# A new table of 61 queue-order pairs in place of 39, in a two-layer hybrid encoder on one core

## The chip, the core and the metric

The kernel runs on one core of a Trainium2 chip. The core has five instruction streams that run side by side and meet only at semaphores: TensorE (PE, with its weight loads shown apart as PEld), VectorE (DVE), ScalarE (ACT), GpSimd (POOL) and SyncE (SP), which here issues nearly all DMAs. Each stream works strictly in the order in which it was written: an instruction that waits holds up everything behind it on its own engine. The metric is the time of one execution on the device in microseconds; less is better. The time of a kernel is the median of several executions.

## The reference

The program is the trunk of an encoder: 512 tokens (a grid of 8 rows by 64 columns) and 16 meta tokens, width 1024, two layers, float32. Cut to what matters:

```python
def hybrid_layer(x, ...):                       # x: 528 x 1024
    h = rms_norm(x, norm_g)
    qa, ka, va, za, qb, kb, vb, zb, ga, gb = split_cols(h @ w_in)      # 1024 x 5376
    qa = rope(rms_norm(qa)); ka = rope(rms_norm(ka))                   # 8 query heads, 2 key heads
    oa = gqa_attention(qa, ka, va) * silu(za)                          # over all 528 keys
    ob = neighbourhood_attention(qb, kb, vb, rpb) * silu(zb)           # 8 heads, 8 x 16 window + meta keys
    mixed = sigmoid(ga) * (oa @ w_o_attn) + sigmoid(gb) * (ob @ w_o_na)
    return x + mixed @ w_out

def reference(x, meta_tokens, ...):
    h = concat([meta_tokens, x])
    for i in range(2):
        h = hybrid_layer(h, ...)
    return rms_norm(h, final_norm_g)[16:]
```

## The kernel before

**Products.** Features lie on the partitions, tokens on the free axis. Every dense product is made of three matmuls per tile: a weight tile is split into a rounded high part `whi` (a cast on ACT, L291) and the rest `wlo` (a subtraction on POOL, L292), the activations into `hh` and `hl`, and PE adds `whi*hh + whi*hl + wlo*hh` in one PSUM bank (L376 to L378). A chunk of 128 output features takes 24 such matmuls per span of tokens: 256 and 272 columns in layer 0 (tiles named like `pp0_11_256`: layer, chunk, first token), 512 in layer 1. Two banks `pp` take turns. Weight halves of 256 KB come by DMA through five buffers `raw`.

**The two attentions** run in the gaps between these chunks. After each span of a product a counter ticks, and steps that are due at that tick are written into the program. The global attention works in units of one head and 256 queries: scores `S` (L607, L608) in one PSUM tile of two banks, their scaled copy with its maximum on DVE (L889, output `P`), exponentials on ACT (L893), a transposition on DVE and by a DMA to DRAM (`turn`) and back, a split into `pth` (ACT) and `ptl` (DVE, L245), and sums `av` on PE (L957) that close with the meta keys `ga` (ACT L948, POOL L950). The windowed attention works by head: a bias tile of 480 KB is loaded (L1026), scores `Sb` go into the same PSUM tile `S`, DVE adds the bias and takes the extreme (L1042, statistic `stb`), ACT exponentiates (L1044), PE transposes (`ta`, `tb`, `tc`, `tm`, and `vtb`, `vtc` for the values) into two PSUM banks tagged `tp`, ACT and DVE split the results (`tah`/`tal`, `tbh`/`tbl`, `mm`, `na`, `VB`), and PE sums `avb` (L1104, eleven matmuls). `ob` and `oa` are the gated results (L825, L829), `mg` the merge gates, `y` the products with the output projections, `za` and `zb` the SiLU gates, `KA` the stacked keys of the global attention, `KB` and `QB` keys and queries of the windowed one.

**What sets the order.** The kernel is written against a planner: instructions are recorded in program order with their dependences, and the planner lays each engine's queue out by priority and by the times that it expects of each instruction; it adds all semaphores. The order on the chip is fixed then. Three things steer it: a few blocks of high priority, `issue_after` (what the block records comes behind a given instruction on its engine), and the table `BEHIND` with `queue_order` (called at the end, L1320 and on). For each engine, `BEHIND` holds pairs `(a, n, b, m)`: the n-th instruction of that engine (counted from 0 in program order) that writes tile `a` is queued behind the m-th one that writes tile `b`. The pair adds no semaphore; it only binds the order of the queue:

```python
kind = mybir.DependencyInfo(mybir.DependencyClass.NoSync, mybir.DependencyReason.DATA)
for engine, pairs in BEHIND.items():
    for a, n, b, m in pairs:
        tc.add_manual_dep(traced[engine, a, n], traced[engine, b, m].name, kind, reason="queue order")
```

Names of tiles carry their place: `avb0_3` is the sum of layer 0, windowed head 3; `S1_3_0_1` the scores of layer 1, head 3, unit 0, second half of its queries. The profile leaves these numbers out (it prints `avb`, `S`), so an instruction is found there by its place among those of its name.

Of the kernel before, what the change touches and what calls it, by code (L numbers as in the profile page):

```python
# [66 lines left out]
    "Activation": (  # L67
# [3 lines left out]
    ),  # L71
    "DVE": (
# [4 lines left out]
    ),  # L77
# [5 lines left out]
    ),  # L83
    "Pool": (
        ("wl6KB", 1, "gb0", 0), ("wlo0_17_1", 0, "zb0_1", 0), ("wlo1_38_1", 0, "zb1_3", 0),
    ),
    "SP": (
        ("turn1_2_1", 0, "QB1_2a", 0),
    ),
}  # L90

# [1276 lines left out]
```

## Time and profile before

| | us |
|---|---|
| median of 3 runs | 826.21 |
| lowest, highest | 824.33, 827.37 |
| the profiled execution | 826.77 |
| its span, first to last instruction | 824.7 |
| mean clock granted to PE, share of full speed | 0.999 |
| PE / PEld busy in the span | 812.2 / 756.4 |
| DVE / ACT / POOL busy in the span | 511.2 / 474.1 / 419.3 |

The profile shows one execution. A row of the timeline reads: start in us from the span's start, length in us, engine, line of the kernel, operation, output tile <- input tiles, shapes, count, and in brackets the idle time of the engine just before the row and what ended it. Rows of neighbouring instructions of one kind are merged (x3). In the view of waits a row reads: who waited <- for whom, us in total, number of waits, the longest. Matmuls are pipelined, so their lengths overlap; from the start of one to the start of the next is what a matmul takes of PE.

### The profile page before, as it was taken

To read this page: it belongs to the slowest core of one execution; us is meant where nothing else is said; L and a number is where in the kernel's file an instruction comes from. 1 tells how busy PE (TensorE), PEld (TensorE's weight loads), DVE (VectorE), ACT (ScalarE), POOL (GpSimd) and SP (SyncE) were. 2 spreads that over 40 slices of the span, in tenths; PEclk is the share of its full clock that TensorE was granted. 3 is DMA by queue.
4 is the path that set the end of the run, shared out by engine and by line. 5 is a ranking of instruction groups with operands and counts; after the bars stand their busy time and mean duration, and the time that the engine had idled before them with its cause. 6 is when DMAs were issued, how large, how long until landed. Compare 5 with 4: busy or idle time off the path is not lost.

```text
span 824.7 us, 16080 instructions
## 1 busy us (share of the span) xinstructions
PE 812.2 (98%) x5662; PEld 756.4 (92%) x5662; DVE 511.2 (62%) x1152; ACT 474.1 (57%) x1137; POOL 419.3 (51%) x362
## 2 busy tenths in 40 slices
PE   9999999999999999999999999999998999999997
PEld 9999999999999999999988989998987788888886
DVE  7566777796885662455547657676766755343733
ACT  8745677577865664433445557666757756534422
POOL 1654454454553544655754644554635456555841
PEclk9999999999999999999999999999999999999999
DMA  8347474567655563435555575666776455653502
GB/s 296 105 133 214 144 210 138 166 211 196 177 160 175 163 209 116 145 101 171 150 121 138 142 226 157 195 175 173 186 231 156 150 184 155 188 194 100 190 2 103
DMA packets 113249, 134.99 MB, mean 164 GB/s; under 512 B 31889, under 2 KB 66193, under 8 KB 113169
## 3 DMA queue, kind: packets, MB, share of 16 engines
q1 hardware_dynamic: 112448, 132.90, 54.8%
q8 instruction: 45, 0.74, 0.4%
q10 hardware_dynamic: 720, 1.06, 0.3%
q14 instruction: 36, 0.29, 0.1%
HBM read 98.50 MB, written 21.84 MB: 146 GB/s over the span
## 4 chain that ended last, share of the span: by engine, by line
PE 85%; DVE 5%; DMA 3%; ACT 3%; issue 2%; SPq 1%; POOL 0%; POOLq 0%; DVEq 0%; ACTq 0%
PE pp L378 18%; PE pp L376 18%; PE pp L377 18%; PE y L377 4%; PE y L378 4%; PE y L376 3%; PE av L957 3%; PE avb L1104 2%; PE S L607 2%; PE S L608 2%; DMA bias<-in_bias_dram 2%; PE pf L1287 2%; PE pf L1286 2%; PE pf L1288 2%; PE pp L496 2%
## 5 line engine op out<-in xcount | busy, mean ns | idle before, releaser
L292 POOL TENSOR_TENSOR wlo<-raw,whi 128x512 fp32r<-128x512 f32 x210 | 286.6, 1373 | 287.4 <-ACT whi L291 233.2
L376 PE MATMUL pp<-hh,whi 128*128 128x256 f32 (+2 forms) x1040 | 325.2, 313 | 0.0
L378 PE MATMUL pp<-hh,wlo 128*128 128x256 f32 (+2 forms) x1040 | 324.2, 312 | 0.0
L377 PE MATMUL pp<-hl,whi 128*128 128x256 f32 (+2 forms) x1040 | 323.3, 311 | 0.0
L378 PEld LDWEIGHTS pp<-hh,wlo 128*128 128x128 f32 x1040 | 195.8, 188 | 10.3
L377 PEld LDWEIGHTS pp<-hl,whi 128*128 128x128 f32 x1040 | 195.7, 188 | 9.3
L376 PEld LDWEIGHTS pp<-hh,whi 128*128 128x128 f32 x1040 | 195.9, 188 | 8.6
L291 ACT CAST whi<-raw 128x512 fp32r<-128x512 f32 x210 | 128.7, 619 | 110.4 <-PE pp L377 43.1
L950 POOL TENSOR_TENSOR ga<-pm,ga 32x128 fp32r<-32x128 f32 x64 | 39.5, 618 | 70.7 <-ACT ga L948 46.3
L919 DVE STREAM_TRANSPOSE P<-P 128x512 f32<-128x512 f32 x64 | 46.4, 725 | 29.7 <-ACT P L893 29.3
L1183 DVE TENSOR_TENSOR mg<-pp,rbc 128x256 f32<-128x256 f32 (+2 forms) x48 | 24.7, 515 | 47.8 <-PE pp L378 47.2
L889 DVE CUSTOM_DVE_ANT_0 P<-S,r 128x528 f32<-128x528 f32 x64 | 44.8, 701 | 15.2 <-PE S L608 14.7
L245 DVE TENSOR_TENSOR ptl<-P,pth 128x512 fp32r<-128x512 f32 x64 | 50.3, 800 | 4.4 <-ACT pth L244 4.2
L893 ACT ACTIVATE P<-P,st 128x528 f32<-128x528 f32 x64 | 47.2, 737 | 1.7
L1044 ACT ACTIVATE bias<-bias,stb 128x208 f32<-128x208 f32 (+1 forms) x64 | 31.0, 485 | 22.6 <-DVE stb L1042 22.5
L1184 ACT ACTIVATE mg<-mg 128x256 f32<-128x256 f32 (+2 forms) x48 | 23.6, 492 | 28.8 <-DVE mg L1183 28.5
L244 ACT CAST pth<-P 128x512 fp32r<-128x512 f32 x64 | 39.2, 613 | 0.5 <-DMA P<-turn 0.4
L377 PE MATMUL pp<-mx,whi 128*128 128x272 f32 (+1 forms) x128 | 36.4, 285 | 0.0
L376 PE MATMUL pp<-mx,whi 128*128 128x272 f32 (+1 forms) x128 | 36.4, 284 | 0.0
L378 PE MATMUL pp<-mx,wlo 128*128 128x272 f32 (+1 forms) x128 | 36.4, 284 | 0.0
L892 ACT ACTIVATE st<-st 128x1 f32<-128x1 f32 x64 | 12.9, 202 | 39.1 <-DVE st L889 38.6
L957 PE MATMUL av<-pth,VA 128*128 128x256 f32 x128 | 34.1, 288 | 0.0
(534 smaller groups left out, 1724.8 us busy)
## 6 DMA issues: line engine op xcount, KB each, us to landing
raw<-in_w_dram SPq DMA_DIRECT2D x210, 256.0 KB
turn<-P SPq DMA_DIRECT2D x32, 528.0 KB
P<-turn SPq DMA_DIRECT2D x128, 128.0 KB
bias<-in_bias_dram SPq DMA_DIRECT2D x16, 480.0 KB
KB<-KB SPq DMA_DIRECT2D x24, 272.0 KB
rawl<-in_w_dram SPq DMA_DIRECT2D x16, 256.0 KB
x<-in_xT_dram SPq DMA_DIRECT2D x8, 264.0 KB
xr<-in_xT_dram SPq DMA_DIRECT2D x8, 264.0 KB
```

Of the source, the lines that this page charges most:

```text
L244: split_at["hi"] = nc.scalar.copy(hi, src)
L245: split_at["any"] = nc.vector.tensor_sub(lo, src, hi.bitcast(F32))
L291: cast = nc.scalar.copy(hi, raw)
L292: sub = nc.gpsimd.tensor_sub(lo, raw, hi.bitcast(F32))
L376: nc.tensor.matmul(ps, wh, rh[:, a:b], start=i == 0, stop=False)
L377: nc.tensor.matmul(ps, wh, rl[:, a:b], start=False, stop=False)
L378: nc.tensor.matmul(ps, wl, rh[:, a:b], start=False, stop=i == n - 1)
L889: newest["max"] = nc.vector.tensor_tensor_reduce(p[:n], joined(S)[:n], scale[:n].to_broadcast([n, NTOK]), 1.0, -3e38, ALU.mult, ALU.max, s ...
L893: nc.scalar.activation(p[:n], p[:n], AF.Exp, bias=st[:n, 1:2], scale=1.0, accum_out=st[:n, 2:3] if total is None else total)
L919: nc.vector.transpose(c["both"][:n, a:b], c["both"][:n, a:b])
L950: nc.gpsimd.tensor_sub(tm[64 + 32 * t:96 + 32 * t, n * t:n * (t + 1)], m, tm[:32, :n].bitcast(F32))
L957: nc.tensor.matmul(c["av"], rows2(c["t"][i][0]), c["t"][i][1], start=i == 0, stop=i == 8)
```

## The change

The table `BEHIND` is replaced by one of 61 pairs, made over three cases of durations of the instructions. All 39 pairs of the old table stand in the new one; 22 are new (8 on PE, 7 on DVE, 5 on POOL, 1 on ACT, 1 on SP). Nothing else is changed: the same instructions, tiles and DMAs. The new pairs are:

```diff
     "Activation": (
+        ("st0_2_1_1", 0, "whi0_13_1", 0),
     "DVE": (
+        ("KA1l1", 0, "P1_0_0", 0), ("VB20_0", 1, "qr0_1", 1), ("mg1_34_5", 0, "ptl1_5_1_0", 0),
+        ("ob0_2", 4, "mm0", 12), ("ptl0_1_0_0", 0, "kb0_2", 0), ("q0_3", 2, "ob0_3", 3),
+        ("za1_3", 0, "ptl1_3_1_0", 0),
     "PE": (
+        ("S1_3_0_1", 0, "avb1_3", 4), ("S1_3_0_1", 0, "avb1_3", 5), ("av1_2_1", 1, "pp1_17_256", 9),
+        ("avb0_3", 6, "pp0_8_0", 3), ("avb0_3", 9, "S0_2_1_1", 1), ("sm0_7", 0, "pp0_35_256", 0),
+        ("tc0_0", 0, "pp0_19_0", 15), ("vtc0_0", 0, "pp0_11_256", 19),
     "Pool": (
+        ("KB1_20", 0, "za1_0", 0), ("ga0", 7, "wlo0_20_1", 0), ("ga0", 51, "wlo1_36_1", 0),
+        ("ga0", 52, "wlo1_36_1", 0), ("wlo0_21_0", 0, "ga0", 10),
     "SP": (
+        ("Q20_1", 2, "KB0_11", 0),
```

More of the change, by code (lines that the diff above doesn't have):

```diff
@@ L69 @@
         ("mg0_26_0", 0, "pth0_6_1_0", 0), ("mg1_26_2", 0, "ga0", 64), ("na0", 6, "pth0_1_1_2", 0),
[1 row of a table removed]
[2 rows of a table added]
     ),
     "DVE": (
[4 rows of a table removed]
[5 rows of a table added]
     ),
     "PE": (
[4 rows of a table removed]
[7 rows of a table added]
     ),
     "Pool": (
-        ("wl6KB", 1, "gb0", 0), ("wlo0_17_1", 0, "zb0_1", 0), ("wlo1_38_1", 0, "zb1_3", 0),
+        ("KB1_20", 0, "za1_0", 0), ("ga0", 7, "wlo0_20_1", 0), ("ga0", 51, "wlo1_36_1", 0), ("ga0", 52, "wlo1_36_1", 0),
+        ("wl6KB", 1, "gb0", 0), ("wlo0_17_1", 0, "zb0_1", 0), ("wlo0_21_0", 0, "ga0", 10), ("wlo1_38_1", 0, "zb1_3", 0),
     ),
     "SP": (
-        ("turn1_2_1", 0, "QB1_2a", 0),
+        ("Q20_1", 2, "KB0_11", 0), ("turn1_2_1", 0, "QB1_2a", 0),
     ),
```

23 rows, old and new, of the table BEHIND are left out of this document.

## The prediction, made before the change was run

> **What bounds the kernel now.** I read the page of the profile first, then the view of who waited for whom, limited to TensorE (PE), then the timeline around each place that the new table touches.
>
> ```profile
> span 824.7 us, 16080 instructions
> PE 812.2 (98%) x5662; PEld 756.4 (92%) x5662; DVE 511.2 (62%) x1152; ACT 474.1 (57%) x1137; POOL 419.3 (51%) x362
> ```
>
> PE is busy for 812.2 of 824.7 us and no other engine passes 62%. An order of instructions can't make a matmul shorter, so all that it can win lies in the 12.5 us in which PE stands still. The waits view (line, what it waited for, us in total, times, longest) splits them:
>
> ```profile
> PE S L607 <- DVE stb L1042: 2.7, 2, 2.1
> PE warm L188 <- DVE one L194: 1.1, 1, 1.1
> PE y L377 <- DVE ob L245: 0.7, 1, 0.7
> PE y L377 <- DVE oa_3b L245: 0.4, 1, 0.4
> PE avb L1104 <- DVE na L850: 0.4, 2, 0.3
> PE tm L180 <- DVE tal L245: 0.4, 1, 0.4
> PE vtc L791 <- DVE tal L245: 0.3, 1, 0.3
> PE avb L1104 <- ACT tbh L244: 0.3, 1, 0.3
> PE S L607 <- DVE st L889: 0.2, 1, 0.2
> ```
>
> That is 6.5 us, 1.1 of them before the first matmul; the other 6.0 are the tail behind the last matmul and what rounding leaves, and no pair touches the tail. So 5.4 us, in 10 waits, are within reach. Each costs a little more than its idle time: the profile draws a matmul of 256 columns 0.28 long while the next one starts 0.12 later (rows below: 573.70 to 573.81), so a wait of w delays PE by w + 0.16. Ten waits make 5.4 + 1.6 = 7.0 us, and one that shows only at the weight load (first place below) adds 0.3: **7.3 us, 0.9%, is all that any order could take away here.**
>
> **The change part by part.** No instruction is added or removed. All 39 old pairs stay and 22 come in: 8 on PE, 7 on DVE, 5 on POOL, 1 on ACT, 1 on the DMA queue of SP. I followed each new pair (a behind b) to its two instructions: in every one a now stands ahead of b, by 1 to 16 instructions. So each asks for a local move. Five of them meet a wait.
>
> First place: the transposes vtc of head 0 (vtc0_0) go 8 matmuls back, behind pp0_11_256 number 19. They wait for a PSUM bank that DVE's tal frees.
>
> ```profile
> 92.43 0.28 PE L377 MATMUL pp<-hl,whi 128*128 128x272 f32 x1
> 92.78 0.27 PEld L791 LDWEIGHTS vtc<-ident,vb 128*80 128x80 f32 x3 [0.29 <-PE pp L378]
> 92.81 0.50 PE L791 MATMUL vtc<-ident,vb 128*80 128x128 f32 x3
> ```
>
> Start to start is 0.38 where 0.12 is the pace: 0.26 is lost. Eight matmuls are 8 x 0.12 = 1.0 us of ready work, so the wait goes: **-0.26**. Queued behind vtc0_0 are the transposes tb and tc; what they make, with VB, is read by avb, which the chain of work has at
>
> ```profile
> 103.09 1.22 PE avb L1104 x11
> ```
>
> so 1 us later is hidden by some 9 us. The move of tc0_0 (16 matmuls) and of VB20_0 on DVE is under the same cover: nothing.
>
> Second place: avb0_3 number 6 goes behind four matmuls of pp0_8_0, and its number 9 behind scores of the next unit.
>
> ```profile
> 156.51 0.28 PE L377 MATMUL pp<-hl,whi 128*128 128x256 f32 x1
> 156.65 0.35 ACT L244 CAST tbh<-tb 80x256 fp32r<-80x256 f32 x1
> 157.05 0.44 PE L1104 MATMUL avb<-tbh,VB 80*128 80x128 f32 x2 [0.26 <-ACT tbh L244]
> ```
>
> 0.54 from start to start, 0.42 lost; tbh is ready at 157.0 and four matmuls are 0.48: **-0.42**. The tail of avb0_3 then ends some 2 us later, and its collection on ACT and DVE with it; PE reads that product only in the y products after all eight heads: nothing.
>
> Third place: on DVE the product ob0_2 (L829) goes behind the copy mm0 number 12.
>
> ```profile
> 160.92 0.71 DVE L829 TENSOR_TENSOR ob<-ob,zb 128x528 f32<-128x528 f32 x1
> ...
> 210.84 1.53 POOL L292 TENSOR_TENSOR wlo<-raw,whi 128x512 fp32r<-128x512 f32 x1 [0.18 <-ACT whi L291]
> 211.15 1.78 DVE L829 TENSOR_TENSOR ob<-ob,zb 128x528 f32<-128x528 f32 x1
> 211.40 0.27 PE L180 MATMUL tm<-ident,pm 128*32 128x128 f32 x1
> 212.97 0.43 DVE L1183 TENSOR_TENSOR mg<-pp,rbc 128x256 f32<-128x256 f32 x1
> 213.31 0.15 DVE L1071 CAST mm<-tm 32x16 fp32r<-32x16 f32 x1
> 215.24 0.67 DVE L245 TENSOR_TENSOR tal<-ta,tah 128x512 fp32r<-128x512 f32 x1
> 216.06 0.50 PE L791 MATMUL vtc<-ident,vb 128*80 128x128 f32 x3 [0.32 <-DVE tal L245]
> ```
>
> The same shape takes 0.71 at 160.92 and 1.78 here, where it began 0.31 behind a POOL operation and ended 0.56 after that one's end (212.37). PE's vtc stood 0.32 + 0.16 = 0.48 for tal, which is late in DVE's queue. With the new order mg and mm (sources in PSUM, ready at 211.2 and 211.7) run in the time in which ob is held up, ob still ends near 212.93, and what follows starts at 213.0 instead of 213.4: **-0.4**. From the other side, if 1.78 is ob's own need here, it starts at 211.9 and ends at 213.7, and tal is 0.3 later: +0.3. I take the first, because the 0.71 row is the nearest of its shape; both ends go into the range. The Trainium skill ("SBUF — State Buffer", section "Who interferes with whom") says that a VectorE instruction with two SBUF inputs and a GpSimd instruction that reads SBUF share one port pair, and that the second to start is blocked until the first is done. By that rule the sum is -1.6, without it -0.9; the end 0.56 behind POOL's agrees with it. The same rule also speaks against such a table: a moved DVE instruction can land behind a POOL one. The fourth place is such a case.
>
> Fourth place: on DVE KA1l1 goes behind the first score evacuation of layer 1, P1_0_0.
>
> ```profile
> 473.78 0.29 PE L608 MATMUL S<-KA1l,Q 128*128 128x272 f32 x1
> 474.00 1.37 DVE L598 TENSOR_TENSOR KA1l<-k,KA1h 64x544 fp32r<-64x544 f32 x1
> 475.40 0.71 DVE L889 CUSTOM_DVE_ANT_0 P<-S,r 128x528 f32<-128x528 f32 x1
> 475.69 0.28 PE L378 MATMUL pp<-hh,wlo 128*128 128x256 f32 x1
> 476.17 0.39 PE L607 MATMUL S<-KA1h,Q 128*128 128x256 f32 x1 [0.21 <-DVE st L889]
> 485.31 0.28 PE L607 MATMUL S<-KA1h,Q 128*128 128x256 f32 x1
> ```
>
> The scores are done at 474.07, but their evacuation stands behind the 1.37 of KA1l. Ahead of it, it ends near 474.8 and the next scores find their bank free: 476.17 - 475.69 - 0.12 = 0.36, **-0.36**. KA1l then ends near 476.2, or by 1.37 more if POOL holds it up, and behind it on DVE come evacuations of vb and the second P; the next scores that need that bank start at 485.31, 8 us later. Its own reader is the second key head, later still. Cover enough.
>
> Fifth place: S1_3_0_1 goes behind numbers 4 and 5 of avb1_3.
>
> ```profile
> 572.26 0.28 PE L1104 MATMUL avb<-tal,VB 128*128 128x256 f32 x1
> 573.11 0.38 PE L607 MATMUL S<-KA1h,Q 128*128 128x256 f32 x1 [0.57 <-DVE stb L1042]
> 573.70 0.28 PE L1104 MATMUL avb<-tal,VB 128*128 128x256 f32 x1
> 573.81 0.46 PE L1104 MATMUL avb<-tbh,VB 128*128 128x256 f32 x3
> ```
>
> The wait costs 0.85 - 0.12 = 0.73. Two matmuls pass in front, each 0.11 at the pace, with inputs that ACT and DVE made before they stood idle: **-0.2**. The rest of the wait, 0.5, stays.
>
> The other moves (sm0_7, av1_2_1, the remaining DVE pairs, the five POOL pairs, st0_2_1_1 on ACT, Q20_1 on SP) have no wait of PE at their place. A gain can't be had there; a cost can, if what is moved back is then late: above nothing, up to a wait like the nine rows, 0.2 to 0.7 each. I take nothing and keep 2 us for the range. Q20_1's DMA on SP passes one key copy that was behind it and is read tens of us later.
>
> **Sum**: 0.26 + 0.42 + 0.4 + 0.36 + 0.2 = 1.64 us. The profiled execution took 826.77 us, its span and 2.07 around it, which would become 825.1. The median of the three runs is 826.21, 0.56 below it, so **824.6 us** for a median.
>
> **The rivals.** (1) *The gains are absorbed*: PE arrives earlier and waits that much longer for something not driven by it. For it: two waits of PE hang on loads of the bias (480 KB each), and their rows say how:
>
> ```profile
> 566.67 4.86 DMA bias<-in_bias_dram
> ...
> 628.99 8.25 DMA bias<-in_bias_dram
> ```
>
> ```profile
> 571.65 0.38 DVE L1042 CUSTOM_DVE_ANT_0 bias<-Sb,bias 128x208 f32<-128x208 f32 x1 [2.28 <-DMA bias<-in_bias_dram]
> ...
> 637.37 0.38 DVE L1042 CUSTOM_DVE_ANT_0 bias<-Sb,bias 128x208 f32<-128x208 f32 x1 [2.02 <-DMA bias<-in_bias_dram]
> ```
>
> Against: these loads are issued after work that PE itself released, so they move with it. Time: 826.2. With it goes the case that the table doesn't do what it says because an instruction's place is set by something else; that the 22 orders are not met now speaks against that.
>
> (2) *More is won than the five places*: the planner places everything behind a moved instruction anew, and the big waits (S for stb, 2.1 + 0.16; y for ob, 0.7 + 0.16) shrink as well. Nothing in the table names them. With both gone: 824.6 - 2.26 - 0.86 = 821.5.
>
> (3) *Slower: the bias loads land later.* The place is DVE's L1042 in layer 1; no slack is left there, since DVE stands 2.28 and 2.02 us for the load and PE's scores wait for DVE, so each us of landing costs PE one us. The same 480 KB took 4.86 in one row and 8.25 in the other: 3.4 between them. If two heads' loads are pushed so behind other transfers by the new order of POOL (wlo1_36_1 is moved right at 629, and frees the buffer of a weight load), the time is 824.6 + 2 x 3.4 = 831.4. It decides from 5.8 us on (4.1 for 0.5%, and the 1.64 won). Against: one pair alone is on SP, and it is in layer 0.
>
> **How the numbers follow.** Forecast 0.50; absorbed or without effect 0.25; more won 0.15; bias loads late 0.10. The low end, 821.6, is (2); the high end, 828.4, is the median plus 2 us of new small waits, with most of (3) left out. About 0.5% is what a measurement of this kernel can tell from no change. Faster by over 0.5% means under 822.1: most of (2) and a little of the forecast, 0.14. Slower by that means over 830.3: part of (3), 0.06. The rest, 0.80, is within.
>
> **What would show it.** Right: PE's busy time stays 812; the rows avb for tbh and vtc for tal go from its waits, S for st L889 goes, S for stb shrinks by 0.2; ob0_2 takes less than 1.78 or starts after mm. Wrong: new rows of over 0.5 us among PE's waits, a bias load that lands over 9 us after its issue, or a wait for wlo. If PE's waits sum to under 4 us or over 9, the places were not what decided.

## The result, and the profile after

| | before | with the new table | the new table again |
|---|---|---|---|
| median, us | 826.04 (22 runs) | 823.10 (22 runs) | 823.87 (12 runs) |
| lowest to highest | 824.21 to 829.17 | 821.64 to 827.00 | 821.60 to 827.84 |
| ratio to before, 95% interval | | 0.9964 [0.9953, 0.9974] | 0.9980 [0.9964, 0.9996] |
| profiled execution, its span | 826.77, 824.7 | 822.95, 820.9 | 825.5, 823.4 |

The kernel became a little faster, by 2.9 us in the first set of runs and 1.9 in the later one, against 1.64 foretold; the median lies inside the predicted range and within half a per cent of before. The third column is a later set of runs of the same program, with its own runs of before (median 825.72).

The page of the profile after, and PE's waits in it (waited <- for whom: us in total, times, longest):

```profile
span 820.9 us, 16081 instructions
PE 810.2 (99%) x5662; PEld 755.1 (92%) x5662; DVE 507.0 (62%) x1152; ACT 474.7 (58%) x1137; POOL 418.8 (51%) x362
```

```profile
PE S L613 <- DVE stb L1048: 1.6, 1, 1.6
PE warm L194 <- DVE one L200: 1.1, 1, 1.1
PE y L383 <- DVE ob L251: 0.7, 1, 0.7
PE y L383 <- DVE oa_3b L251: 0.4, 1, 0.4
PE pp L502 <- ACT hh L397: 0.3, 1, 0.3
PE avb L1110 <- DVE na L856: 0.3, 1, 0.3
PE tm L186 <- DVE tal L251: 0.2, 1, 0.2
PE avb L1110 <- ACT tbh L250: 0.2, 1, 0.2
```

(The new table is six lines longer, so L1042 is now L1048.) PE's busy time was to stay at 812 and is 810.2, with the same matmuls: the profile draws a matmul longer than its pace, so about half of the 3.8 us that this execution gained was drawn as busy before. The rows of vtc for tal and of S for st are gone, as foretold; avb for tbh is shorter but still there; y for ob and y for oa_3b are untouched. The row of scores for stb fell from two waits with 2.7 us to one with 1.6. Three of the places, PE first, then POOL and DVE:

```profile
93.09 0.29 PE L383 MATMUL pp<-hl,whi 128*128 128x272 f32 x1
93.22 0.49 PE L797 MATMUL vtc<-ident,vb 128*80 128x128 f32 x3
...
209.68 1.54 POOL L298 TENSOR_TENSOR wlo<-raw,whi 128x512 fp32r<-128x512 f32 x1 [0.18 <-ACT whi L297]
211.14 0.69 DVE L835 TENSOR_TENSOR ob<-ob,zb 128x528 f32<-128x528 f32 x1
...
472.88 1.29 POOL L571 TENSOR_TENSOR qb<-qb,QB_0b 128x512 fp32r<-128x512 f32 x1
472.98 1.78 DVE L604 TENSOR_TENSOR KA1l<-k,KA1h 64x544 fp32r<-64x544 f32 x1
```

At the first place vtc now starts 0.13 behind the matmul ahead of it, at the pace. At the third, ob starts as POOL's wlo ends (211.22) and takes 0.69 for the 1.78 of before. At the fourth the opposite happened: KA1l now starts 0.10 behind a POOL operation and takes 1.78 where it took 1.37, with the P that mattered already out of its way.

**Where the time went, step by step.** Both programs have the same number of PE instructions, so the start of the n-th matmul after can be set against that of the n-th before, and the difference cut into stretches (us, negative is a gain; times are those of before):

| stretch | foretold | new table | again |
|---|---|---|---|
| 0 to 11, first loads | 0 | -0.07 | -0.47 |
| 91 to 108, first place (vtc0_0) | -0.26 | -0.28 | -0.28 |
| 124 to 139, tm0_2 | 0 | -0.18 | -0.18 |
| 139 to 154, av for ptl | 0 | -0.39 | -0.39 |
| 154 to 164, second place (avb0_3) | -0.42 | -0.10 | -0.21 |
| 173 to 193 | 0 | -0.13 | -0.14 |
| 209 to 222, third place (ob0_2) | -0.40 | -0.48 | -0.48 |
| 241 to 251, y for ob | 0 | -0.23 | -0.20 |
| 474 to 487, fourth place (KA1l1) | -0.36 | -0.47 | -0.47 |
| 571 to 582, fifth place and a bias load | -0.20 | -0.90 | -0.05 |
| 582 to 596 | 0 | +0.20 | +0.20 |
| 635 to 643, a bias load | 0 | -0.53 | +1.42 |
| all others | 0 | -0.27 | -0.10 |
| whole span | -1.64 | -3.83 | -1.35 |

Two executions of one program, 2.5 us apart, agree within 0.03 in most rows. Three rows differ by more than 0.2: the start, and the two stretches that hold the waits for a bias load, called the *bias windows* below. (Within "all others", the second execution has one wait of avb for na at 237 that the first has not, 0.25.) Without these three rows the change gained **2.33 and 2.25 us**.

### The profile page after: what moved, and what is told of

It is laid out like the page before. It is cut to its first block, busy times and chain, and to the rows that moved or that the text cites. A ratio compares the mean times of both kernels' runs of the same rounds, so it can differ in the third digit from the quotient of the medians.

```text
span 820.9 us, 16081 instructions
## 1 busy us (share of the span) xinstructions
PE 810.2 (99%) x5662; PEld 755.1 (92%) x5662; DVE 507.0 (62%) x1152; ACT 474.7 (58%) x1137; POOL 418.8 (51%) x362
## 4 chain that ended last, share of the span: by engine, by line
PE 93%; DMA 2%; DVE 2%; ACT 1%; issue 1%; POOL 0%; SPq 0%; POOLq 0%; ACTq 0%; DVEq 0%
PE pp L384 20%; PE pp L383 20%; PE pp L382 20%; PE av L963 4%; PE y L383 4%; PE y L384 4%; PE y L382 4%; PE avb L1110 2%; PE S L613 2%; PE S L614 2%; PE pf L1293 2%; PE pf L1292 2%; PE pf L1294 2%; PE pp L502 1%; DMA bias<-in_bias_dram 1%
## 5 line engine op out<-in xcount | busy, mean ns | idle before, releaser
L251 DVE TENSOR_TENSOR ptl<-P,pth 128x512 fp32r<-128x512 f32 x64 | 47.9, 762 | 4.4 <-ACT pth L250 4.2
```

The costliest lines, as they stand in the source:

```text
L251: split_at["any"] = nc.vector.tensor_sub(lo, src, hi.bitcast(F32))
```

## The experiments

Twelve kernels ran, in three sets of four; the kernel before ran beside each set (medians 825.61, 825.72 and 826.39).

**Which pairs do it (first set).** One pair alone; the new table without it; the old table and the nine pairs of the five places; the old table and the twelve others.

```diff
 e1_za:    old table
+    "Pool": ("KB1_20", 0, "za1_0", 0)
 e2_no_za: new table
-    "Pool": ("KB1_20", 0, "za1_0", 0)
 e3_five:  old table
+    the new pairs of vtc0_0, tc0_0, VB20_0, avb0_3 (two), ob0_2, KA1l1, S1_3_0_1 (two)
 e4_rest:  old table
+    the new pairs of st0_2_1_1, mg1_34_5, ptl0_1_0_0, q0_3, za1_3, av1_2_1, sm0_7, ga0 (three), wlo0_21_0, Q20_1
```

> The old table with one pair added: on POOL the key split KB1_20 queued behind the product za1_0. The planner then changes nothing but the order of these two instructions. Theory A (the pair that the prediction costed at nothing): za is ready some 1.8 us earlier at 545, so DVE's oa (L829) begins without waiting and ends about 1.3 us earlier, the chain of queries QB_2 and the bias load behind it issue about 0.4 us earlier, and PE's wait for stb at 572 shrinks from 0.57 idle to about 0.1; PE is 0.4 to 0.6 us earlier from 580 on, and the median about 0.5 us under that of before. Rival B (the bias load lands when it lands, the gain at 572 was chance of one execution): the wait at 572 stays between 0.4 and 0.7 and the median does not move.

> The new table without that one pair; again only these two instructions on POOL change places. Theory A: the wait for stb at the score of layer 1, head 3 comes back, less the two matmuls in front, to 0.3 to 0.4 us of idle (0.5 of loss), and the median is about 0.5 us over that of the changed kernel, near 823.6. Rival B: no row for it, median as the changed kernel.

> The old table and only the nine pairs of the five places that the prediction costed (vtc0_0, tc0_0, VB20_0; avb0_3 twice; ob0_2; KA1l1; S1_3_0_1 twice). The prediction's sum: 1.64 us under before, ratio about 0.998. If the gain of 0.36% came mainly from elsewhere, this one shows it by falling short of about half of it: 1.5 us or less. In the profile: the waits vtc for tal and S for st L889 gone, avb for tbh at most 0.26, S for stb at 572 at about 0.4.

> The old table and the twelve pairs that stand at no wait of PE (st0_2_1_1; mg1_34_5, ptl0_1_0_0, q0_3, za1_3; av1_2_1, sm0_7; ga0 three times, wlo0_21_0; Q20_1). The prediction's account: nothing, 0 to 2 us slower. Theory C, from the comparison of the two profiles: ptl0_1_0_0 lets DVE make tal 0.2 us earlier for the transpose tm at 128, q0_3 takes a wait of y for ob at 243 away (0.2), the rest nothing, so 0.4 us faster, ratio 0.9995; the bias load at 629 is as before within 0.5 us.

| | median | ratio, 95% interval | gain in its profile outside start and bias windows |
|---|---|---|---|
| e1_za | 828.02 | 1.0021 [1.0005, 1.0038] | 0.12 |
| e2_no_za | 823.21 | 0.9971 [0.9957, 0.9985] | 1.84 |
| e3_five | 826.11 | 0.9999 [0.9984, 1.0015] | 1.27 |
| e4_rest | 824.68 | 1.0001 [0.9986, 1.0016] | 0.63 |

(The ratio is the record's own estimate; for e4_rest the two medians alone would give 0.9989.) Neither forecast for e1_za came true: its wait for stb at 572 grew from 0.57 to 1.09 us, and its median rose. The median of e2_no_za lies between the two that were forecast for it, 823.6 and 823.10, and decides nothing. By their medians e3_five and e4_rest gain much less than the new table does.

The medians and the profiles don't fit together. The nine pairs of e3_five gain 1.33 us at the first four of their places, and the median shows nothing. (The 1.27 of the table comes about otherwise: 0.39 more is gained at av for ptl, told in the last section, and 0.46 is lost at 164 to 173, where DVE's ob took 1.29 for 0.70 behind an operation of POOL.) One pair whose profile loses nothing over 0.1 in any other place costs 2.3 us. Something that no place shows weighs more than the places. The profile of e1_za lost 0.5 in the first bias window and 1.8 in the second, against before.

**Is it the bias windows? (second set).** The new table unchanged; the new table with a bias load sent ahead of two weight loads; the new table with the scores that wait put behind ready matmuls; and that with seven more such moves.

```diff
 e5_again:      new table, nothing changed
 e6_bias_first: new table
+    "SP": ("raw1_37_1", 0, "bias1_7", 0), ("raw1_46_0", 0, "bias1_7", 0)
 e7_hide:       new table
+    "PE": ("S1_5_0_1", 0, "pp1_36_0", 23), ("S1_5_0_1", 0, "avb1_6", 10),
+          ("S1_3_0_1", 0, "avb1_3", 10), ("S1_3_0_1", 0, "pp1_17_0", 3)
 e8_more:       e7_hide
+    "PE": ("tm0_2", 0, "pp0_16_256", 21), ("avb0_3", 6, "pp0_8_0", 6), ("avb0_7", 0, "av0_4_0", 6),
+          ("avb1_5", 0, "pp1_9_0", 1), ("avb1_7", 0, "pp1_37_0", 17),
+          ("y00_42_0", 10, "y00_42_256", 8), ("y01_46_0", 10, "S1_5_1_1", 3)
```

> The new table, unchanged, once more: the same kernel as the one after the change. Theory A (the gains of the places are fixed; what varies from one execution to the next is how late two bias loads of layer 1 land, the one before the scores at 572 and the one before those at 635): outside these two windows each step repeats within 0.1 us of what the first profile of this kernel showed against the profile of before (place 1 -0.28, the tm transposes near 128 -0.18, the av sums at 152.5 -0.39, place 3 -0.48, y for ob at 243 -0.23, place 4 -0.47), while PE's wait of scores for stb, 1.6 us there, comes out elsewhere between 0 and 3.5; the times fall in two groups some 3 us apart, median 822.5 to 824.5. Theory B (the order sets the bias waits too, and with them the whole 3 us): stb is 1.6 again within 0.3 and at the same place, and the times form one group.

The table above has the steps: theory A held, and stb was 2.8 us in two waits. More than the wait differs. The scores behind it, in the repeat and in before:

```profile
636.17 0.58 PE L613 MATMUL S<-KA1h,Q 128*128 128x256 f32 x1 [2.07 <-DVE stb L1048]
```

```profile
638.83 0.39 PE L607 MATMUL S<-KA1h,Q 128*128 128x256 f32 x1 [2.12 <-DVE stb L1042]
```

Stretches of the trace round the second window, first of the repeat, then of before (start:end, length, busy time of each engine, then the clock granted to PE as a share of full speed, DMA share, GB/s):

```profile
634.50:636.00 1.50, 0.00 (x0) 0.00 (x0) 1.28 (x7) 0.87 (x3) 0.12 (x1) 1.00 0.54 155
636.00:637.50 1.50, 1.33 (x5) 1.33 (x6) 0.16 (x3) 1.16 (x6) 0.00 (x0) 0.52 0.05 18
637.50:639.00 1.50, 1.50 (x5) 1.11 (x5) 1.00 (x4) 0.76 (x2) 0.00 (x0) 0.50 0.00 0
639.00:640.50 1.50, 1.50 (x13) 1.50 (x12) 0.69 (x1) 0.89 (x3) 0.00 (x0) 0.84 0.03 3
```

```profile
637.50:639.00 1.50, 0.17 (x1) 0.18 (x2) 1.27 (x8) 1.21 (x5) 0.00 (x0) 1.00 0.53 146
639.00:640.50 1.50, 1.50 (x10) 1.32 (x11) 0.85 (x4) 0.94 (x5) 0.00 (x0) 1.00 0.06 23
```

In the repeat PE stood for 2.07 us and then worked for about 3 us at half the clock: the matmuls of 512 columns there start 0.43 apart instead of 0.23, and the stretch from 635 to 643 lost 1.42 against before. In before PE had stood for 2.12 and kept its clock. In e1_za it stood for 2.4 and lost it too, 1.1 us after it had begun to work again:

```profile
640.50:642.00 1.50, 1.50 (x7) 1.27 (x6) 1.21 (x5) 0.92 (x4) 0.00 (x0) 0.56 0.01 4
```

So a wait of this length sometimes costs 1.4 us more than itself. When it does can be read from the trace, which records each change of the granted clock. In the repeat the clock goes to full at 4.588 us and to half at 636.053; in e1_za at 5.796 and 640.675. These spans are 185 and 186 times 3.413 us, and both stretches at half speed last 3.413 us. So the changes come at ticks that far apart, counted from the first full speed, which falls 4.0 to 7.3 us after the start in the 14 profiles. The step that ended with the drop held 1.95 us without a drawn matmul in the repeat and 2.36 in e1_za. In before a tick at 638.61 cut the wait of 2.12, and the step that ended there held 1.91: no drop. Behind the last matmul all 14 profiles drop as well, always at a tick: first after a step with 2.08 us or more of idle time, never after one with 1.79 or less. In these profiles the limit lies between 1.91 and 1.95 us in one step, and where the ticks fall decides what a wait of 2 us costs. The Trainium skill ("TensorE: Matmul & The Clock Gate", "Part 1: The HAM clock gate") says that the clock is halved after a window of about 3.4 us without work, and that the window runs freely; the trace agrees on the half pace, on the length of the step and on its running freely, but 1.95 us without work in a step was enough.

Each execution's mean granted clock is on record. One such stretch, 3.4 us at half speed, takes about 0.002 off it (an estimate: 1.7 of 824 us). The drop behind the last matmul costs no time, but in the 14 profiles it took up to 0.0022 off too, so 0.998 can come from that alone, and 0.997 or less did not. That splits the runs:

| | executions | with clock 0.997 or less | their median | median of the others |
|---|---|---|---|---|
| before (three sets) | 93 | 15 | 828.06 | 825.42 |
| new table (both sets) | 34 | 8 | 825.59 | 823.08 |
| e1_za | 12 | 7 | 828.98 | 825.74 |
| e2_no_za | 12 | 2 | 825.98 | 822.76 |
| e3_five | 12 | 5 | 827.21 | 824.43 |
| e4_rest | 12 | 5 | 827.71 | 824.41 |
| e6 to e8 | 36 | 0 | | 822.58, 824.73, 823.31 |
| e9 to e12, below | 34 | 2 | 826.97, 827.17 | 825.07, 824.61, 821.56, 820.82 |

Only two of the executions at 0.997 or less were profiled, the repeat and e1_za, and both lost the clock in the second window; that the others lost it there is inferred. Among the executions above 0.997, the new table gains 825.42 - 823.08 = 2.3 us, which is what the places sum to. The medians of e1_za, e3_five and e4_rest are those of a mixture: with 5 to 7 of 12 executions at the lower clock, they say more of that share than of the pairs. The other executions of e3_five and e4_rest are 1.0 us under those of before in the same set (825.46). The share itself differs between sets (before: 3 of 35, 3 of 35 and 9 of 23), so it is to be compared within a set.

> The new table and two pairs on SP: the two weight loads (256 KB each) that stand 1.3 and 0.9 us ahead of the bias load of head 7 in layer 1 go behind it. Theory A1 (the two weight loads ahead make the bias load late): from issue to the first use on DVE falls from 7.8 us to 5 to 6, PE's wait of 1.8 at 633 goes to under 0.3, the profile is 1.5 us and the median 1 to 1.5 us under the new table's (821.5 to 822). Theory A2 (what makes it late is behind it: the loads of P in many small packets, or the chip's memory itself): 7 to 8 us again, wait and time as with the new table, within 0.5 us. On the other side: the weights come late by more than their buffer's slack, a wait of pp for whi or wlo appears, and the time is 0.5 to 1.5 us longer.

822.58 (821.89 to 824.81), ratio 0.9963 [0.9953, 0.9973]. SP's queue and DVE's first use of the load, in the profile of the new table and in that of e6_bias_first:

```profile
624.46 1.21 SPq L292 DMA_DIRECT2D raw<-in_w_dram  x2
625.78 0.41 SPq L1032 DMA_DIRECT2D bias<-in_bias_dram  x1
...
633.61 0.38 DVE L1048 CUSTOM_DVE_ANT_0 bias<-Sb,bias 128x208 f32<-128x208 f32 x1 [1.67 <-DMA bias<-in_bias_dram]
```

```profile
625.63 0.38 SPq L1037 DMA_DIRECT2D bias<-in_bias_dram  x1
626.11 1.28 SPq L297 DMA_DIRECT2D raw<-in_w_dram  x2
...
632.83 0.37 DVE L1053 CUSTOM_DVE_ANT_0 bias<-Sb,bias 128x208 f32<-128x208 f32 x1 [0.58 <-PE Sb L619]
```

With the two weight loads behind it, DVE no longer waits for the load but for its scores (the releaser is PE's Sb). PE's wait at 633 is gone, and no execution is left in the lower clock group. The median is 1.3 us under that of the new table in the same set (823.87), as theory A1 has it, but not at its 821.5 to 822. The 5 to 6 us of the expectation can't be read here, since DVE's start, 7.2 us after the issue, is set by the scores. In the other window PE still waited 1.6 us for stb in this profile.

> The new table and four pairs on PE: the scores S1_5_0_1 (which waited 1.6 us for stb) go behind the 4 matmuls left of pp1_36_0 and the 11 of avb1_6 (0.94 + 1.2 = 2.1 us of work), and S1_3_0_1 behind the rest of avb1_3, three transposes and 4 matmuls of pp1_17_0 (some 1.4 us). The loads stay where they are. Theory A: PE's row of scores for stb goes or falls under 0.4, the profile gains 1.4 to 1.8, the median 1 to 2 us (821 to 822), and the two groups of times come together, the highest run under 825, since a late bias load now meets ready work. Rival: the groups come from something else (another wait, the clock); then the profile gains the same 1.4 to 1.8 but the groups stay 3 us apart. On the other side: what reads these scores is late by the 2 us, and a wait of av for pth or ptl, or of S for st, takes the gain back.

824.73, ratio 0.9998 [0.9983, 1.0013]: no gain over the new table, though stb is gone from PE's waits. Its first rows are now:

```profile
PE av L968 <- ACT pth L255: 1.3, 1, 1.3
PE y L388 <- DVE ob L256: 1.1, 1, 1.1
...
PE avb L1115 <- DVE na L861: 0.8, 2, 0.5
PE y L388 <- DVE oa_3b L256: 0.4, 1, 0.4
PE av L968 <- DVE ptl L256: 0.4, 1, 0.4
```

The forecast of 821 to 822 failed, and the third case of the expectation came: the wait goes on to pth, and to ob and na of a later head. In the first window, DVE, then ACT and PE:

```profile
574.79 0.56 DVE L256 TENSOR_TENSOR VB<-vtb,VB 128x384 fp32r<-128x384 f32 x1 [2.11 <-ACT VB L255]
575.26 0.70 DVE L900 CUSTOM_DVE_ANT_0 P<-S,r 128x528 f32<-128x528 f32 x1
...
576.00 0.20 ACT L903 ACTIVATE st<-st 128x1 f32<-128x1 f32 x1 [1.25 <-DVE st L900]
576.98 0.60 ACT L255 CAST pth<-P 128x512 fp32r<-128x512 f32 x1
577.63 0.39 PE L968 MATMUL av<-pth,VA 128*128 128x256 f32 x1 [1.33 <-ACT pth L255]
```

The moved scores are done near 573.2. Their copy P stands in DVE's queue behind VB, which waited 2.11 us for ACT; with the new table P had stood ahead of VB. So ACT gets st only at 576.0, and pth stands in ACT's queue behind st and the exponentials. ACT is busy right up to pth, so it isn't the loads of P that pth waited for. At the second window the same kind of move did better in this profile: 635 to 643 is 2.36 shorter than before, and 0.65 of that is lost again by 660, for na and ob. To put a waiting instruction behind ready work hides the wait of that instruction only; what reads its result comes later with it, and so does what is queued behind those readers. (No execution is in the lower clock group, and yet the times run from 822.12 to 828.21: the clock is not the whole of the spread.)

> The table of the run before it (four pairs for the two waits for stb) and seven more, one for each further wait of PE of over 0.25 us in the profile of the new table: tm0_2, avb0_3 number 6, avb0_7, avb1_5, avb1_7 and the two y products go behind 0.2 to 0.8 us of ready matmuls. These places lost 0.36, 0.32, 0.26, 0.29, 0.41, 0.57 and 0.85 there. Theory A (a wait put behind ready work gives back its loss, as at places 1, 3 and 4): all but 0.35 of these 3.06 come back, 2.0 to 2.8 us under the run before it in profile and median (818.5 to 820). Rival (absorbed: PE comes earlier and waits longer at the next): under 1 us.

823.31, ratio 0.9976 [0.9963, 0.9989]: 1.4 under e7_hide, below the 2.0 to 2.8 of theory A and above the rival. In its profile tm0_2, the y product at 332 and avb1_5 gained 0.27, 0.30 and 0.40 against the new table's profile; avb0_3 and avb0_7 nothing; and at 641, just ahead of avb1_7, stands a new wait of 1.3 us of tc for tal, after a bias load that took 8.0 us to its first use.

**Do the gains add up once the windows are closed? (third set).** The two SP pairs on the old table, on the old table with the pair of e1_za, on the new table with the other bias load sent ahead too, and that with the three moves that had kept their gain.

```diff
 e9_old_bf:   old table
+    "SP": ("raw1_37_1", 0, "bias1_7", 0), ("raw1_46_0", 0, "bias1_7", 0)
 e10_za_bf:   e9_old_bf
+    "Pool": ("KB1_20", 0, "za1_0", 0)
 e11_bias4:   e6_bias_first
+    "SP": ("sumsb1_1", 0, "bias1_4", 0), ("sumsb1_1", 1, "bias1_4", 0)
 e12_more_bf: e11_bias4
+    "PE": ("tm0_2", 0, "pp0_16_256", 21), ("avb1_5", 0, "pp1_9_0", 1), ("y00_42_0", 10, "y00_42_256", 8)
```

> The old table and the two SP pairs that put two weight loads behind the bias load of head 7 in layer 1. In the profile of before PE lost 2.28 at 636 for that load. Theory A (the new table's gains outside the two bias windows, 2.3 us in both of its profiles, are there whatever the windows do): the loss at 636 goes, and the time is that of the new table with the same two pairs (822.6) plus 2.3, so 824.9 within 0.5; before's median then held a loss of only 0.8 at 636. Theory B (the windows are what the new table gained on, and the gains of its places are absorbed by them): 2.3 under before's 825.7, so 823.4 or less.

> The old table, the pair of KB1_20 behind za1_0 on POOL, and the two SP pairs. Without the SP pairs that one pair made the old table 2.3 us slower (828.0), though its profile showed no step outside the bias windows over 0.1. Theory A (its 2.3 us are the window at 636, where its profile lost 1.8 more than before): as the run before it within 0.6 (824.3 to 825.5). Theory B (the pair costs elsewhere, or at 572): 827 or more, and its profile shows where.

> The new table, the two SP pairs, and two more that put the loads of sumsb (1.2 us of SP) behind the bias load of head 4 in layer 1, whose buffer is free by then. In four profiles of kernels with all or most of the new table PE lost 0 to 1.7 at 570 for it. Theory A: the load lands 1.2 us earlier against PE, the loss at 570 falls to 0 to 0.5, the time to 821.4 to 822.2. Rival, from the run in which the scores were put behind ready work (there PE lost 1.5 at 576 for pth instead): the loads of P behind the bias load are as late, PE's wait goes to pth, and the time is the 822.6 of the SP pairs alone, within 0.4. On the other side: sumsb comes late for POOL's gate zb, which holds up POOL's weight halves behind it: 0.5 to 1.5 longer, with a wait of pp for wlo.

> As the run before it, and the three pairs on PE (of the seven tried) after whose place the profile kept a gain: tm0_2 (-0.27 against the new table), the y product y00_42_0 (-0.30) and avb1_5 (-0.40, of which a wait of av for ptl at 614 gave 0.3 back). Theory A: 0.6 to 1.0 under the run before it, 820.6 to 821.4 if that one is at 821.4 to 822.2, and the fastest of all. Rival (absorbed): within 0.3 of it.

| | median | lowest to highest | ratio, 95% interval |
|---|---|---|---|
| e9_old_bf | 825.11 | 823.75 to 826.97 | 0.9984 [0.9971, 0.9998] |
| e10_za_bf | 824.65 | 824.01 to 827.70 | 0.9983 [0.9967, 0.9998] |
| e11_bias4 | 821.56 | 821.07 to 821.98 | 0.9940 [0.9920, 0.9960] |
| e12_more_bf | 820.82 | 820.50 to 821.21 | 0.9933 [0.9916, 0.9951] |

Theory A held four times by the medians. With the same two SP pairs, new against old table is 825.11 - 822.58 = 2.5 us. The two ran in different sets; each taken against before in its own set (3.1 and 1.3 us lower), it is 1.9. The pair that alone cost 2.3 us costs nothing once the window at 636 is closed, so its price lay in that window. And with both windows closed the spread of 5 to 6 us falls to 0.9 and 0.7 (in five executions each, against 12 or more). The profiles are less even than the medians: in e9_old_bf the wait of tm for tal at 129, which the new table shortens, is 1.2 us for the 0.4 of before, and in e11_bias4 a wait of 0.7 of tc for tal stands at 639. Of the three moves of e12_more_bf the profile keeps 0.26 at tm0_2 and 0.30 at the y product; the 0.37 of avb1_5 is lost again some 8 us on, at av for ptl. The waits of PE in e12_more_bf are short enough to show whole:

```profile
PE warm L200 <- DVE one L206: 1.1, 1, 1.1
PE y L389 <- DVE ob L257: 0.7, 1, 0.7
PE pp L508 <- ACT hh L403: 0.6, 1, 0.6
PE avb L1116 <- DVE na L862: 0.2, 1, 0.2
```

This version is faster than both kernels: 820.82 against 823 to 824 and about 826 (the new table alone did not run in this set).

## Why the prediction was right, and where its sum was not

**The method** held: the time moved through PE's waits and, past a limit, through its clock. The bound of 7.3 us counts only waits that the view draws, but nothing here went past it: e12_more_bf gained 6.3 in its profile.

**First, third and fourth place**: foretold 0.26, 0.40 and 0.36, measured 0.28, 0.48 and 0.47. At the third the choice between two readings of a 1.78 row came out for the shorter need: ob takes 0.69 when POOL's operation ends as it starts. DVE gained more there than the 0.4 of the sum (tal starts 2.86 earlier, where PE's matmuls before it are 1.2 earlier), so PE got back its whole wait of 0.48. At the fourth, KA1l began 0.10 behind a POOL operation and took 1.78, where its like took 0.72 at 470.44. The cover that the text counted (8 us to the next scores) took it.

**Second place**: foretold 0.42, measured 0.10 and 0.21. The step that failed is "tbh is ready at 157.0 and four matmuls are 0.48". The pair puts avb behind number 3 of pp0_8_0, but numbers 0 and 1 stood ahead of it already; the two rows of the profile quoted there show only the last of them. Two matmuls are 0.24, and in the first profile even that was not won: 0.32 of the 0.42 stayed, since PE came 0.95 earlier than in before and ACT's work ahead of tbh only 0.79.

**The moves costed at nothing** were the mis-sized term. Outside the places the first profile shows 1.0 us: gains of 0.18 at tm, 0.39 at av for ptl, 0.23 at y for ob and 0.13 near 176, a loss of 0.20 near 589, and 0.24 in small steps late. The first three, 0.8 us, stand in e4_rest too, which has these pairs without the five places (and loses 0.29 at the second place). The two near 176 and 589 stand in neither half alone, and 0.19 of small late steps stand in e1_za as well, so these can't be put down to the moves. The step that failed was "have no wait of PE at their place. A gain can't be had there". One was a listed wait whose cause stood one step back in DVE's queue: tm waited for tal, and the pair of ptl0_1_0_0 takes a split from ahead of it. DVE in before, then after:

```profile
126.66 0.68 DVE L245 TENSOR_TENSOR ptl<-P,pth 128x512 fp32r<-128x512 f32 x1
...
128.50 0.68 DVE L245 TENSOR_TENSOR tal<-ta,tah 128x512 fp32r<-128x512 f32 x1
```

```profile
127.31 0.68 DVE L251 TENSOR_TENSOR tal<-ta,tah 128x512 fp32r<-128x512 f32 x1
...
128.52 0.68 DVE L251 TENSOR_TENSOR ptl<-P,pth 128x512 fp32r<-128x512 f32 x1
```

Another was a loss that the waits view can't list, since the profile draws a matmul longer than its pace, as the prediction itself had said. In before:

```profile
243.68 0.28 PE L376 MATMUL y<-ob,whi 128*128 128x256 f32 x1
243.97 0.39 PE L377 MATMUL y<-ob,whi 128*128 128x256 f32 x1
```

0.29 from start to start where 0.12 is the pace, and no idle time drawn. It was won back with the twelve other pairs (-0.21 in e4_rest, -0.01 in e3_five). The third, av for ptl, is a race between two engines, told below.

**Fifth place**: 0.2 was foretold and can't be told apart. The bias load arrives when it arrives; in the first profile of the new table PE didn't wait there at all, in the second 0.7 us.

**The rivals.** "Absorbed" didn't come true for the change, but it is what e7_hide ran into. "More is won" was half right in size and wrong in its reason: y for ob stayed at 0.7, and stb shrank in one execution and not in the next. "Bias loads late" named the right place; its driver, the new order of POOL, isn't shown. Both tables have a spread from execution to execution there, and the one pair of e1_za, on POOL, made the long case more frequent in the old table. Its price of one us per us was too low: at about 2 us a wait can cost 1.4 us more through the clock. The forecast treated the 2.7 us of stb in one profile as a fixed quantity of the kernel; it is a draw. (The range's ends are given as 821.6 and 828.4; the terms named for them make 821.5 and 828.2.)

## What to carry to other kernels

Before an order is judged by its median, look at whether the executions fall into groups, and set the granted clock of each beside its time: a wait near the length at which the clock can drop turns a small shift into 1.4 us more, and the groups here stand 2.5 to 3.3 us apart. Profile one program twice and compare the starts of the same instruction; what repeats is likely the change's, what doesn't is a wait for something with a spread of its own. Cure such a wait at its source where that can be done: putting the waiting instruction behind ready work moved the wait on (e7_hide), and sending the late load ahead of others on its queue removed it (e6_bias_first, e11_bias4).

## What was not expected of the hardware

**A wait of 2.1 us of PE can halve its clock** for 3.4 us, and one of the same length need not (2.07 with, 2.12 without). In these profiles it turned on how much of one step of 3.413 us the wait filled: 1.95 us or more with, 1.91 or less without.

**To start 0.03 us behind POOL cost DVE 1.1 us.** In two kernels with the old table, e9_old_bf and e10_za_bf, the same two operations, POOL's zb and DVE's ptl, meet at 150.8. First e9_old_bf, then e10_za_bf:

```profile
150.79 1.29 POOL L875 TENSOR_TENSOR zb<-zb,sumsb 128x512 f32<-128x512 f32 x1 [1.58 <-DMA sumsb<-thereb]
150.82 1.81 DVE L246 TENSOR_TENSOR ptl<-P,pth 128x512 fp32r<-128x512 f32 x1
```

```profile
150.54 0.68 DVE L247 TENSOR_TENSOR ptl<-P,pth 128x512 fp32r<-128x512 f32 x1
150.81 1.57 POOL L876 TENSOR_TENSOR zb<-zb,sumsb 128x512 f32<-128x512 f32 x1 [1.89 <-PE tc L182]
```

The one that starts second is held up, whichever it is: 1.81 for 0.68 on DVE, 1.57 for 1.29 on POOL. That agrees with the Trainium skill ("SBUF — State Buffer", "Who interferes with whom"). PE's sums wait for ptl: the stretch from 139 to 154 is 0.39 shorter in e10_za_bf than in before. Of the four profiles with the old order at that place, POOL was first in three (before, e1_za, e9_old_bf). In the nine with the new table's twelve other pairs POOL stood longer before zb (2.5 to 4.7 us for 1.5 to 1.9), and zb began 0.9 to 3.1 us after ptl did; in e3_five 0.6. So the gain of 0.39 is the new table's as far as these profiles go, though the old order had it once by luck; which pair holds zb back was not tried.

**One 480 KB load took 6 to 8.6 us from its issue to DVE's first use** at 629, behind the same two loads of 256 KB (8.38 before, 7.83 and 8.29 with the new table, 8.60 in e1_za; in e4_rest DVE came 6.17 after the issue and did not have to wait). Why it varies, and why the lone pair of e1_za made the long case more frequent (7 of 12 executions at the lower clock, against 3 of 35 of before in the same set), stays open; the third set shows only that the cost lay in that window.
